# SwiGLU products by one level of Strassen's recursion in a two-layer decoder step

## The chip, the cores and the metric

The kernel runs on one core of one Trainium2 chip. The metric is the device time of one execution in microseconds; the median of three runs is taken.

## The reference, cut to what matters

One inference step of a two-layer decoder for 1024 prompt tokens and 8 x 8 sample tokens, model width 1024, all in float32. Layer 0 mixes tokens by trailing means over 2 to 16 positions, layer 1 by dilated attention in three branches over a shared K/V. Each layer ends with a SwiGLU:

```python
def _swiglu(h, w_gate, w_up, w_down):
    return (jax.nn.silu(h @ w_gate) * (h @ w_up)) @ w_down
...
        xp = xp + _swiglu(_rmsnorm(xp, ffn_norm[layer]), w_gate[layer], w_up[layer], w_down[layer])
        xs = xs + _swiglu(_rmsnorm(xs, ffn_norm[layer]), w_gate[layer], w_up[layer], w_down[layer])
```

The hidden width D_FF is 2816. The caches of the sample tokens are also copied to the outputs, shifted by the new rows.

## The kernel before, in words

The engines are TensorE (PE, whose weight loads are shown as PEld), VectorE (DVE), ScalarE (ACT), GpSimd (POOL) and SyncE (SP, which issues most DMAs). Prompt and sample tokens stand side by side as T = 1088 columns. The residual stream `xall` is kept feature-major, 8 tiles of 128 features by 1088 tokens.

Every float32 operand of a large product is split (`split`, L195) into a high part, ACT's cast to fp32r (L196), and a low part, DVE's subtraction (L197). `mm3` (L199) makes a product of three matmuls from them: high x high, high x low, low x high (L200 to L202). Each matmul loads its own 128 x 128 weights.

A SwiGLU (`ffn`, L358) runs over 22 chunks of 128 hidden features and, inside, over the three token groups of 364, 362 and 362 columns in `GROUPS`. `load` brings a chunk's gate, up and down weights and splits them. `gate_up` (L373) makes 2 x 8 products into two PSUM banks, then ACT's Silu (L384), DVE's product (L385) and a split of the result. `down` (L391) makes eight products, one for each 128 output features, and DVE adds each from PSUM onto `xall` (L399). `norm` (L317) makes the normed stream of a group: ACT squares, DVE adds (L332), a matmul with ones, the reciprocal root, DVE's scaling (L353) and a split. Layer 0's norm of a group is called by the pool mixer as soon as that group is mixed, and its last groups are split for the projections (`split_stream`, L431) while others still run. The output projection (L1000 to L1008) goes over the same three groups.

The order on an engine is made by a scheduler from the program's order and its own costs, except on POOL within a SwiGLU, where it is the program's. `copy_some` (L163) has POOL issue the next cache copies (168 in all, about 1 MB each, HBM to HBM); each waits for the last matmul made before it. In the SwiGLUs before, POOL does nothing else. In attention POOL has products of its own (L902) and casts (L754).

SBUF holds three raw weight tiles (`raw_tile`) and twelve split ones (`split_tile`, `wide_tile`); PSUM's eight banks are shared by tags (`FFN_PS`: s 3, p 2, o 1, a 2).

## Time and profile before

| what | us |
|---|---|
| median of the three runs | 3244.33 |
| lowest, highest run | 3237.19, 3258.73 |
| span of the profiled execution | 3241.6 |

The profile is of one execution. Its span goes from the first to the last instruction; no other time of that execution is given, and the three runs lie on both sides of it. Matmuls are pipelined: their records overlap, so the time that one costs is read from how many start in a stretch, not from the length of a record. By stage: the pool mixer to about 85 us, the first SwiGLU to 907, the projections to 1756, attention to 2330, the output projection to 2422, the second SwiGLU and the outputs to the end.

### The profile page before, as it was taken

Reading aid. Unit: us, or ns where it says so; the run is one execution under the profiler, and the core shown is the slowest. Engines: PE = TensorE matmul, PEld = TensorE weight load, DVE = VectorE, ACT = ScalarE, POOL = GpSimd, SP = SyncE. Lnnn points to the kernel's source line nnn. Section 1 sums busy time; section 2 is a strip of 40 time slices with the busy share of each in tenths; the row PEclk is TensorE's granted clock in tenths of the full one; section 3 lists DMA queues with packets and bytes.
Section 4 is the critical chain, followed back from the end, with each engine's and each line's share of the span. In section 5 each row is a group of like instructions: output and inputs, shape, how many; then the busy total and the mean of one; then the engine's idle time right before and its main releaser. Section 6 shows DMA issues by size and latency. Waiting matters only on the chain.

```text
span 3241.6 us, 50563 instructions
## 1 busy us (share of the span) xinstructions
PE 3191.2 (98%) x18673; PEld 2943.7 (91%) x18673; DVE 2144.0 (66%) x4692; ACT 1194.6 (37%) x3907; POOL 207.4 (6%) x463
## 2 busy tenths in 40 slices
PE   8999999999999999999998999999999999999998
PEld 7999999999978888888887888888999999999998
DVE  6655555555689999799892677687636555555555
ACT  5311111111255565253442677777523111111111
POOL 1000000000000000000000012132100000000000
PEclk9999999999999999999998999999999999999999
DMA  4444454445446676978977667776424455445431
GB/s 131 151 162 159 152 172 162 160 149 175 143 146 203 229 226 215 323 266 289 317 218 204 181 225 253 232 260 213 167 67 149 156 175 163 148 155 173 160 118 56
DMA packets 250140, 599.75 MB, mean 185 GB/s; under 512 B 24190, under 2 KB 128174, under 8 KB 246069
## 3 DMA queue, kind: packets, MB, share of 16 engines
q1 hardware_dynamic: 216167, 368.89, 36.3%
q0 software_dynamic: 5376, 174.60, 15.4%
q10 hardware_dynamic: 28350, 53.03, 4.5%
q8 instruction: 147, 2.41, 0.3%
q14 instruction: 100, 0.82, 0.1%
HBM read 534.51 MB, written 243.56 MB: 240 GB/s over the span
## 4 chain that ended last, share of the span: by engine, by line
PE 96%; DVE 2%; DMA 1%; ACT 1%; issue 0%; SPq 0%; DVEq 0%; ACTq 0%
PE ps_s L200 9%; PE ps_s L202 9%; PE ps_s L201 9%; PE ps_p L201 8%; PE ps_p L200 8%; PE ps_p L202 8%; PE ps_o L200 5%; PE ps_o L201 5%; PE ps_o L202 5%; PE ps_a L201 4%; PE ps_a L200 4%; PE ps_a L202 4%; PE ps_s L827 4%; PE ps_o L860 3%; PE ps_p L852 2%; PE ps_a L757 2%
## 5 line engine op out<-in xcount | busy, mean ns | idle before, releaser
L399 DVE TENSOR_TENSOR xall<-xall,ps_s 128x362 f32<-128x362 f32 (+1 forms) x1056 | 546.3, 531 | 582.2 <-PE ps_s L202 575.8
L196 ACT CAST wsplit<-wraw 128x1024 fp32r<-128x1024 f32 x142 | 149.0, 1050 | 654.5 <-PE ps_s L201 270.8
L200 PE MATMUL ps_p<-yah,wsplit 128*128 128x362 f32 (+1 forms) x1104 | 363.5, 329 | 0.2
L201 PE MATMUL ps_p<-yal,wsplit 128*128 128x362 f32 (+1 forms) x1104 | 362.6, 330 | 0.6 <-DVE yal L197 0.4
L202 PE MATMUL ps_p<-yah,wsplit 128*128 128x362 f32 (+1 forms) x1104 | 362.7, 329 | 0.0
L200 PE MATMUL ps_s<-hh,wsplit 128*128 128x362 f32 (+1 forms) x1056 | 349.5, 332 | 6.6 <-DVE xall L399 4.0
L201 PE MATMUL ps_s<-hl,wsplit 128*128 128x362 f32 (+1 forms) x1056 | 348.4, 330 | 0.0
L202 PE MATMUL ps_s<-hh,wsplit 128*128 128x362 f32 (+1 forms) x1056 | 348.3, 330 | 0.0
L200 PE MATMUL ps_o<-yah,wsplit 128*128 128x362 f32 (+1 forms) x752 | 248.4, 330 | 0.0
L201 PE MATMUL ps_o<-yal,wsplit 128*128 128x362 f32 (+1 forms) x752 | 247.3, 329 | 0.0
L202 PE MATMUL ps_o<-yah,wsplit 128*128 128x362 f32 (+1 forms) x752 | 247.1, 329 | 0.0
L201 PEld LDWEIGHTS ps_p<-yal,wsplit 128*128 128x128 f32 x1104 | 208.5, 189 | 1.7 <-DVE yal L197 1.6
L200 PEld LDWEIGHTS ps_p<-yah,wsplit 128*128 128x128 f32 x1104 | 209.0, 189 | 0.5 <-ACT yah L196 0.4
L202 PEld LDWEIGHTS ps_p<-yah,wsplit 128*128 128x128 f32 x1104 | 208.8, 189 | 0.0
L200 PEld LDWEIGHTS ps_s<-hh,wsplit 128*128 128x128 f32 x1056 | 199.0, 189 | 10.1 <-DVE xall L399 6.7
L197 DVE TENSOR_TENSOR wsplit<-wraw,wsplit 128x1024 fp32r<-128x1024 f32 x142 | 173.5, 1222 | 41.0 <-ACT wsplit L196 40.9
L202 PEld LDWEIGHTS ps_s<-hh,wsplit 128*128 128x128 f32 x1056 | 200.0, 189 | 0.0
L201 PEld LDWEIGHTS ps_s<-hl,wsplit 128*128 128x128 f32 x1056 | 199.8, 189 | 0.2
L384 ACT ACTIVATE sl<-ps_p 128x364 f32<-128x364 f32 (+1 forms) x132 | 62.3, 472 | 324.0 <-PE ps_p L202 324.0
L838 ACT ACTIVATE S<-S,ml 128x128 f32<-128x128 f32 (+1 forms) x384 | 169.1, 443 | 28.3 <-DVE ml L833 26.1
L167 POOL DMA_DIRECT2D out_kv_sample<-in_cache_kv_w x168 | 81.6, 488 | 1518.2 <-PE ps_o L202 1054.1
L196 ACT CAST hh<-sl 128x364 fp32r<-128x364 f32 (+1 forms) x132 | 65.3, 494 | 302.7 <-PE ps_s L202 260.6
(290 smaller groups left out, 7486.2 us busy)
## 6 DMA issues: line engine op xcount, KB each, us to landing
sqb<-q SPq DMA_DIRECT2D x128, 512.0 KB
vc<-in_cache_kv_w SPq DMA_DIRECT2D x208, 256.0 KB
skt<-in_cache_kv_w SPq DMA_DIRECT2D x96, 512.0 KB
wraw<-in_w_kv SPq DMA_DIRECT2D x48, 512.0 KB
out_kv_sample<-in_cache_kv_w POOLq DMA_DIRECT2D x24, 960.0 KB, 7.5
wraw<-in_w_gate SPq DMA_DIRECT2D x44, 512.0 KB
wraw<-in_w_up SPq DMA_DIRECT2D x44, 512.0 KB
wraw<-in_w_down SPq DMA_DIRECT2D x44, 512.0 KB
```

The source lines that it names most:

```text
L167: c = bulk.dma_start(_raw(kv_s[b], (n * WIN[b] + r) * row, [[row, m], [1, row]]), _raw(caches[b], (n * WIN[b] + r + TS) * row, [[row, m], ...
L196: nc.scalar.copy(h, x)
L197: nc.vector.tensor_sub(l, x, h.bitcast(FT))
L200: nc.tensor.matmul(out, wh, xh, start=first, stop=False)
L201: nc.tensor.matmul(out, wh, xl, start=False, stop=False)
L202: mark[0] = nc.tensor.matmul(out, wl, xh, start=False, stop=last).ins
L399: nc.vector.tensor_add(xT[m][:, o:o + n], xT[m][:, o:o + n], p[:, :n])
L757: nc.tensor.matmul(acc, w, vl, start=e == 0, stop=False)
L827: nc.tensor.matmul(ps[hh][:, c:c + 128], self.qT[hs, jj, :], kt[hs, jj, :], start=True, stop=True)
L838: nc.scalar.activation(subs[hh][:, e], subs[hh][:, e], AF.Exp, bias=self.ml[:, 0, h:h + 1], scale=-1.0, accum_out=self.ml[:, 1, h:h + 1])
L852: nc.tensor.transpose(pp[:, e * 128:(e + 1) * 128], Sf[:, e * 128:(e + 1) * 128], ident)
L860: nc.tensor.matmul(self.po[:, h % 8 * 64:h % 8 * 64 + 64], Ps[hh][:, c:c + 128], vv[:, h * 64:(h + 1) * 64], start=z == 0, stop=z == nb - 1)
```

## The change

With A the weights, transposed, and B the normed stream, cut into 2 x 2 blocks, one level of Strassen's recursion (in Winograd's form) makes the four result blocks from seven block products and sums of blocks. For gate and up, A is cut by pairs of hidden chunks (11 pairs) and by halves of the features, B into forms of 4 x 128 features by 272 tokens. The 1088 tokens are four blocks of NB = 272; blocks 0 and 1 are the left half (B11, B21), 2 and 3 the right one, and an index g goes over the two blocks of a half. The forms B11, B21, B22 and T1 to T4 are made once per layer by `forms_one` and `forms_two` and kept split. The forms of A are made for each unit (a pair and "gate" or "up"). The gated blocks are stored to scratch HBM (`hd`) and the SwiGLU's whole gate/up part runs before its down part, which loads them again for each of its seven products and forms sums on POOL. In down, a product fills all eight PSUM banks over 11 chunks, and its result is added to one or more blocks of the stream, which has been stored to HBM before the gate/up part and is loaded again. The down weights are loaded afresh for each product. The cache copies are issued three per unit in gate/up and three at chunks 3 and 7 of each down product, until they are used up.

The projections read the stream back from HBM in tiles and take the token tiles in the order `TORD`, those of blocks 2 and 3 first. The split weight tiles are ten instead of twelve; the projections and the output projection get four of their own. The pool mixer's groups become 384, 384 and 320 tokens, its tiles a pool of their own.

The diff, cut to the new order and the functions that set it:

```diff
-GROUPS = ((0, 364), (364, 362), (726, 362))
+STR_PS = {"f": 8}
+NSPLIT = 10
+NB = T // 4
+NPAIR = NFF // 2
+AHEAD = 3
+TORD = (5, 6, 7, 8, 0, 1, 2, 3, 4)
...
+    def norm(q, gain, tag):
+        w = wide_tile()
+        sq = [w[:, :NB], w[:, NB:2 * NB]]
+        acc = w[:, 2 * NB:3 * NB]
+        for k in range(8):
+            xk = xall[:, k, q * NB:(q + 1) * NB]
+            if k == 0:
+                nc.scalar.activation(acc, xk, AF.Square)
+                continue
+            nc.scalar.activation(sq[k % 2], xk, AF.Square)
+            nc.gpsimd.tensor_add(acc, acc, sq[k % 2])
...
+        r = wide_tile()[:, :NB]
+        nc.scalar.copy(r, p[:, :NB])
+        for k in range(8):
+            xk = xall[:, k, q * NB:(q + 1) * NB]
+            nc.vector.scalar_tensor_tensor(xk, xk, gain[:, k:k + 1], r, op0=OP.mult, op1=OP.mult)
+    def quarter(kh, q):
+        return xall[:, 4 * kh:4 * kh + 4, q * NB:(q + 1) * NB]
+
+    def forms_one(X, g):
+        split(*X["B11", g], quarter(0, g))
+        split(*X["B21", g], quarter(1, g))
+
+    def forms_two(X, g):
+        y11, y12, y21, y22 = quarter(0, g), quarter(0, g + 2), quarter(1, g), quarter(1, g + 2)
+        split(*X["B22", g], y22)
+        nc.vector.tensor_sub(y11, y12, y11)
+        split(*X["T1", g], y11)
+        nc.gpsimd.tensor_sub(y12, y22, y12)
+        nc.vector.tensor_sub(y22, y22, y11)
+        split(*X["T2", g], y22)
+        split(*X["T3", g], y12)
+        nc.gpsimd.tensor_sub(y21, y22, y21)
+        split(*X["T4", g], y21)
...
+    STEPS = ("A11", "A12", "S2", "S3", "S1", "A22", "S4")
+    MATE = {"A11": "B11", "A12": "B21", "S4": "B22", "A22": "T4", "S1": "T1", "S2": "T2", "S3": "T3"}
...
+    def gate_up(layer, X, pl, hd, ncopy):
...
+        def prep(n, f):
+            if n >= len(UNITS):
+                return
+            if f == "A11":
+                load(n)
+            (a11, a21), (a12, a22) = ((r[:, :, 0:128], r[:, :, 128:256]) for r in RAW[n])
+            if f == "S2":
+                s = wide_tile().rearrange("p (z k f) -> p z k f", z=2, k=4)
+                nc.vector.tensor_add(s[:, 0], a21, a22)
+                nc.vector.tensor_sub(s[:, 1], s[:, 0], a11)
+                SUM[n, "S1"], SUM[n, "S2"] = s[:, 0], s[:, 1]
+                s = wide_tile().rearrange("p (z k f) -> p z k f", z=2, k=4)
+                nc.vector.tensor_sub(s[:, 0], a11, a21)
+                nc.vector.tensor_sub(s[:, 1], a12, SUM[n, "S2"])
+                SUM[n, "S3"], SUM[n, "S4"] = s[:, 0], s[:, 1]
+            if f in ("A11", "A12") and n < 2 * EARLY:
+                return
+            src = {"A11": a11, "A12": a12, "A22": a22}[f] if f[0] == "A" else SUM[n, f]
+            F[n, f] = split_form(src)
+        def product(p, n, f, g, first, last):
+            h, l = F[n, f]
+            xh, xl = X[MATE[f], g]
+            for k in range(4):
+                mm3(p[:, :NB], h[:, k], l[:, k], xh[:, k], xl[:, k], first and k == 0, last and k == 3, skip_group_check=True)
+        def take(n, b, g, src, other=None, op=None):
+            c, nm = UNITS[n]
+            if nm == "g":
+                s = SG[c, b][:, g]
+                if other is None:
+                    nc.scalar.activation(s, src, AF.Silu)
+                else:
+                    nc.vector.tensor_tensor(s, other, src, op=op)
+                    if g:
+                        nc.scalar.activation(SG[c, b], SG[c, b], AF.Silu)
+            else:
+                s = SG[c, b]
+                if other is None:
+                    nc.vector.tensor_mul(s[:, g], s[:, g], src)
+                else:
+                    if g == 0:
+                        U[n, "t"] = pl.tile([128, 2, NB], FT, name="ct", bufs=2)
+                    t = U[n, "t"]
+                    nc.vector.tensor_tensor(t[:, g], other, src, op=op)
+                    if g:
+                        nc.gpsimd.tensor_mul(s, s, t)
+                if g:
+                    sync.dma_start(hd[b, c], s.rearrange("p g t -> p (g t)"))
+        def one(n):
...
+            pa = [bank("f") for g in range(2)]
+            for g in range(2):
+                product(pa[g], n, "A11", g, True, True)
+                nc.scalar.copy(u[:, g], pa[g][:, :NB])
+            for g in range(2):
+                product(pa[g], n, "A12", g, False, True)
+                take(n, "B11", g, pa[g][:, :NB])
...
+        def rest(n, j, pb):
...
+                p = pb[g] if f == "S4" else bank("f")
+                if f == "S1":
+                    pb.append(p)
+                product(p, n, f, g, f != "S4", True)
+                s = p[:, :NB]
+                if f == "S2":
+                    nc.vector.tensor_add(u2[:, g], u2[:, g], s)
+                elif f == "S3":
+                    nc.vector.tensor_add(u3[:, g], u2[:, g], s)
+                elif f == "S1":
+                    take(n, "B22", g, s, u3[:, g], OP.add)
+                elif f == "A22":
+                    take(n, "B21", g, s, u3[:, g], OP.subtract)
+                else:
+                    take(n, "B12", g, s, u2[:, g], OP.add)
...
+        for n in range(2 * EARLY):
+            load_early(n)
+        for j in range(7):
+            prep(0, STEPS[j])
+        for n in range(2 * EARLY):
+            one(n)
+            copy_some(ncopy)
+        for n in range(len(UNITS)):
+            pb = []
+            for j in range(7):
+                prep(n + 1, STEPS[j])
+                if j == 0:
+                    if n >= 2 * EARLY:
+                        one(n)
+                    if n >= 2 * EARLY:
+                        copy_some(ncopy)
+                elif j > 1:
+                    rest(n, j, pb)
+    DOWN = (("A11", "B11"), ("S1", "T1"), ("S2", "T2"), ("S4", "B22"), ("S3", "T3"), ("A12", "B21"), ("A22", "T4"))
+    def down(layer, kp, hp, hd, ncopy, after):
...
+        def prep(n):
+            if n >= 7 * NPAIR:
+                return
+            s, c = divmod(n, NPAIR)
+            fa, fb = DOWN[s]
+            if fa == "A11":
+                src = two(s, c, 0, 0)
+            elif fa == "S1":
+                r = wraw(c, 0, 1, 2, 128 * D)
+                src = SK[c] = kp.tile([128, 512], FT, name=f"sk{c}")
+                nc.gpsimd.tensor_add(src, r[:, 0], r[:, 1])
+            elif fa == "S2":
+                src = SK[c]
+                nc.gpsimd.tensor_sub(src, src, two(s, c, 0, 0))
...
+            t = split_tile()
+            W[n] = t[:, :512], t[:, 512:]
+            split(*W[n], src)
+            if fb == "T1":
+                TK[c] = kp.tile([128, 2 * NB], FT, name=f"tk{c}")
+                src = TK[c]
+                nc.gpsimd.tensor_sub(src, hraw("B12", c), hraw("B11", c))
...
+            t = hp.tile([128, 2, 2 * NB], FR, name="hf", bufs=4)
+            Hf[n] = t[:, 0], t[:, 1]
+            split(*Hf[n], src)
...
+        for s, (fa, fb) in enumerate(DOWN):
+            pb = [bank("f") for _ in range(8)]
+            for c in range(NPAIR):
+                n = s * NPAIR + c
+                prep(n + AHEAD)
+                (wh, wl), (xh, xl) = W.pop(n), Hf.pop(n)
+                for i in range(4):
+                    for g in range(2):
+                        m, t = slice(i * 128, i * 128 + 128), slice(g * NB, (g + 1) * NB)
+                        mm3(pb[2 * i + g][:, :NB], wh[:, m], wl[:, m], xh[:, t], xl[:, t], c == 0, c == NPAIR - 1)
+                if c in (3, 7):
+                    copy_some(ncopy)
+            for i in range(4):
+                for g in range(2):
+                    p, u = pb[2 * i + g][:, :NB], uu[:, 2 * i + g]
+                    x11, x12, x21, x22 = (xall[:, i + 4 * z, (g + 2 * t) * NB:(g + 2 * t + 1) * NB]
+                                          for z in range(2) for t in range(2))
+                    if fa == "A11":
+                        nc.scalar.copy(u, p)
+                        nc.gpsimd.tensor_add(x11, x11, u)
+                    elif fa == "S1":
+                        nc.vector.tensor_add(x22, x22, p)
+                        nc.vector.tensor_add(x12, x12, p)
+                    elif fa == "S2":
+                        nc.vector.tensor_add(u, u, p)
+                        nc.gpsimd.tensor_add(x12, x12, u)
...
+            if fa == "S3":
+                after(1)
+            elif fa == "A22":
+                after(0)
+    def swiglu(layer, X, xa, xs, npool, last, after):
...
+        with pool("g1") as pl:
+            gate_up(layer, X, pl, hd, 3)
+        npool.close()
+        xa.close()
...
+            for q in (0, 2, 1, 3):
+                sync.dma_start(blk(xall, q), xs[q])
+            down(layer, kp, hp, hd, 3, after)
+            last()
...
+    def mixed(gi):
+        if gi == 1:
+            spill("x0", (0, 1), x0)
+            for g in range(2):
+                norm(g, G_F0, "s")
+                forms_one(X, g)
...
+    spill("x0", (2, 3), x0)
+    X.update(form_tiles(xb.enter_context(pool("xb", side="left")), ("B22", "T1", "T2", "T3", "T4")))
+    for g in range(2):
+        norm(g + 2, G_F0, "s")
+        forms_two(X, g)
+    xr.close()
+    psum_shares(STR_PS)
+    swiglu(0, X, xa, x0, xb, lambda: None, lambda half: spill("x1", (2 * half, 2 * half + 1), x1))
...
-        for o, n in GROUPS:
+            for q in range(4):
+                t = slice(q * NB, (q + 1) * NB)
...
+                if m4 and q < 2:
+                    spill("x2", (q,), x2)
+                    norm(q, G_F1, "s")
+                    forms_one(X, q)
...
```

## Rows read from the trace of the kernel before

**Rows 1.** The page: busy time by engine, and the chain by engine.

```profile
PE 3191.2 (98%) x18673; PEld 2943.7 (91%) x18673; DVE 2144.0 (66%) x4692; ACT 1194.6 (37%) x3907; POOL 207.4 (6%) x463
...
PE 96%; DVE 2%; DMA 1%; ACT 1%; issue 0%; SPq 0%; DVEq 0%; ACTq 0%
```

**Rows 2.** Windows by stage; the columns are named in the first line.

```profile
core 0: us, PE busy (x) PEld busy (x) DVE busy (x) ACT busy (x) POOL busy (x), PEclk, DMA share, GB/s
85.00:112.00 27.00, 25.64 (x136) 24.18 (x136) 23.82 (x52) 14.70 (x28) 0.67 (x1) 0.88 0.37 117
112.00:150.00 38.00, 38.00 (x233) 37.99 (x232) 21.08 (x47) 12.33 (x22) 2.43 (x5) 1.00 0.51 166
150.00:870.00 720.00, 720.00 (x4345) 720.00 (x4344) 378.02 (x664) 119.41 (x185) 39.67 (x82) 1.00 0.49 161
870.00:907.00 37.00, 30.14 (x148) 25.93 (x148) 34.95 (x52) 13.11 (x16) 0.00 (x0) 0.91 0.33 105
...
2422.00:2428.00 6.00, 0.81 (x8) 0.73 (x7) 4.92 (x16) 5.09 (x9) 0.00 (x0) 0.88 0.53 157
2428.00:2460.00 32.00, 31.42 (x172) 30.40 (x172) 30.28 (x75) 18.22 (x39) 1.04 (x2) 0.86 0.20 67
2460.00:3180.00 720.00, 720.00 (x4346) 720.00 (x4345) 374.73 (x659) 118.45 (x184) 37.77 (x78) 1.00 0.47 154
3180.00:3241.60 61.60, 51.89 (x331) 49.55 (x329) 34.32 (x67) 9.04 (x16) 0.00 (x0) 0.98 0.19 73
```

**Rows 3.** Windows of the projections, same columns.

```profile
1100.00:1700.00 600.00, 600.00 (x2644) 490.95 (x2643) 552.52 (x1093) 277.38 (x1380) 0.00 (x0) 1.00 0.78 262
1500.00:1700.00 200.00, 200.00 (x882) 163.68 (x881) 182.95 (x306) 83.64 (x363) 0.00 (x0) 1.00 0.84 285
```

**Rows 4.** Groups by line and shape, whole span: xcount | busy us, mean ns | idle before.

```profile
L399 DVE TENSOR_TENSOR xall<-xall,ps_s 128x362 f32<-128x362 f32 x704 | 363.3, 531 | 415.2 <-PE ps_s L202 410.8
L200 PEld LDWEIGHTS ps_p<-yah,wsplit 128*128 128x128 f32 x1104 | 209.0, 189 | 0.5 <-ACT yah L196 0.4
L197 DVE TENSOR_TENSOR wsplit<-wraw,wsplit 128x1024 fp32r<-128x1024 f32 x142 | 173.5, 1222 | 41.0 <-ACT wsplit L196 40.9
L196 ACT CAST vh<-vc 128x512 fp32r<-128x512 f32 x208 | 122.2, 615 | 60.9 <-DMA vc<-in_cache_kv_w 31.4 <-PE ps_a L758 22.4 <-PE ps_a L757 3.1
L902 POOL TENSOR_TENSOR wraw<-wraw,mw 128x1024 f32<-128x1024 f32 x16 | 32.7, 2063 | 84.6 <-DVE mw L899 84.2 <-DMA mm<-ml 0.4
L353 DVE SCALAR_TENSOR_TENSOR nf<-xall,gcol,nr 128x362 f32<-128x362 f32 x32 | 18.5, 592 | 1.3 <-ACT nr L350 1.1
```

**Rows 5.** Timeline of attention: start us, us, engine line op, xcount.

```profile
2131.55 5.30 DVE L197 TENSOR_TENSOR vl<-vc,vh 128x512 fp32r<-128x512 f32 x3
...
2131.72 4.59 POOL L902 TENSOR_TENSOR wraw<-wraw,mw 128x1024 f32<-128x1024 f32 x2 [0.61 <-DVE mw L899]
...
2201.30 1.98 PEld L860 LDWEIGHTS ps_o<-wsplit,P 128*128 128x128 f32 x16
...
2202.07 0.69 DVE L197 TENSOR_TENSOR vl<-vc,vh 128x512 fp32r<-128x512 f32 x1
...
2202.24 4.60 POOL L902 TENSOR_TENSOR wraw<-wraw,mw 128x1024 f32<-128x1024 f32 x2 [0.45 <-DMA mm<-ml]
2203.09 1.99 DVE L197 TENSOR_TENSOR vl<-vc,vh 128x512 fp32r<-128x512 f32 x1 [0.32 <-ACT vh L196]
...
2205.00 0.41 DVE L833 CUSTOM_DVE_ANT_0 S<-ps_s,amask 128x256 f32<-128x256 f32 x1
```

**Rows 6.** The page: the DMA queue of the cache copies.

```profile
q0 software_dynamic: 5376, 174.60, 15.4%
```

**Rows 7.** Window of the prompt's attention, columns as in the windows above.

```profile
1850.00:2330.00 480.00, 476.12 (x3535) 406.42 (x3534) 359.85 (x1115) 351.18 (x1025) 111.84 (x284) 0.99 0.66 218
```

More of the change, by code (lines that the diff above doesn't have):

```diff
@@ L32 @@
 NVAL = NS * 2 * 13
-NT = 'a'
-ON_PE = False
 TURN = 3
@@ L55 @@
 VALUE_SPAN = 96
-TILES_OF = ((0, 1), (2, 3, 4), (5, 6, 7, 8))
 def _constants():
@@ L1013, in output @@
+    ystack.close()
+    spill("x2", (2, 3), x2)
+    X.update(form_tiles(xb.enter_context(pool("xb1", side="left")), ("B22", "T1", "T2", "T3", "T4")))
+    for g in range(2):
+        norm(g + 2, G_F1, "s")
+        forms_two(X, g)
+    xr.close()
+    psum_shares(STR_PS)
+    def output():
+        for i in TORD:
             o, n = TILES[i]
-            y = pl.tile([128, D], FT, name="y", bufs=3)
+            y = wide_tile()
             for h2 in range(2):
-                p = bank("s" if i > 4 and h2 else "p")
+                p = bank("f")
@@ L1024, in output @@
             sync.dma_start(dst, y[:n])
-    with pool("ffn1") as pl:
-        for gi in range(3):
-            norm(gi, pl, yh, yl, G_F1)
-        ffn(1, yh, yl, pl, (1, 1, 2), lambda gi: output(pl, TILES_OF[gi]))
+    swiglu(1, X, xa, x2, xb, output, lambda half: None)
     copy_some(len(copies_left))
```

439 lines of the change are left out of this document (220 added, 219 removed).

## Prediction

> **What bounds the kernel now.** I read the page's sums first. TensorE (PE) is busy 98% of the span, and the chain that ended last lies 96% on PE [rows 1]. The windows by stage show where: in the two steady SwiGLU stretches PE is busy all of 720.00 us, with 4345 and 4346 matmuls, while VectorE (DVE) is at 52%, ScalarE (ACT) at 17% and the DMA engines at half [rows 2]. So a SwiGLU costs what its matmuls cost, one every 720.00 / 4345 = 165.7 ns, for moving operands of 364, 362 and 362 columns (mean 362.7). The profiled execution's span is 3241.6 us; the median of the three runs, 3244.3, is 2.7 us above it. The sum below is made against the span and 2.7 is added at the end. About 1% (32 us) is what a measurement of this kernel can tell from no change.
>
> **The matmuls, the term with the minus sign.** Before, a layer's SwiGLU has 22 x (16 + 8) products x 3 passes x 3 groups = 4752 matmuls. After: gate and up 22 units x 7 products x 2 token halves x 4 k x 3 passes = 3696, down 7 x 11 chunks x 8 banks x 3 = 1848, together 5544 of 272 columns. Columns fall by an eighth (1,723,392 to 1,507,968), instructions rise by a sixth, so all depends on what one of 272 costs. No row has that size with this type. Two rows span the nearest: 362.7 columns at 165.7 ns, and 512 columns, in the projections, at 600.00 / 2644 = 226.9 ns [rows 3]. The line through them has 0.410 ns a column and 17 ns a matmul; at 272 it gives 128.6 ns. Bounds: 272/362.7 of 165.7, that is 124.3 ns, if all of it scaled, and 165.7 if none did. I take 128.6, since both rows lie on it. Two layers: 9504 x 165.7 = 1574.8 against 11088 x 128.6 = 1425.9 us: **-149**. The output projection goes from three groups to four blocks: 576 x 165.7 = 95.4 to 768 x 128.6 = 98.8: **+3**.
>
> The Trainium skill, "TensorE: Matmul & The Clock Gate", section "Back-to-back issue gap", gives columns / 2.4 + 2.5 ns for a warm matmul by itself. At 272 that would be 115.8 ns, and the sum 142 us lower; but it would also give 153.6 and 215.8 ns for the two sizes above, 11 to 12 ns under both measured ones, so the sum goes by the rows.
>
> **The start of each SwiGLU.** Before, a group's norm is followed by its matmuls. After, only B11 and B21 (token blocks 0 and 1) serve the early products of four units, 4 x 48 x 128.6 ns = 24.7 us of PE work; the rest waits for T1 to T4, which need all four blocks. The work in that wait: per pair of a block of each half, a norm has 7 adds of 272 on POOL and 8 scalings on DVE, and forms_two has 7 DVE operations of 1088 elements and 2 on POOL. From the rows (DVE 531 ns at 362 and 1222 at 1024 elements, 592 for a scaling of 362, POOL 2063 at 1024 [rows 4]) these are 7 x 0.55 + 8 x 0.50 + 7 x 1.29 + 2 x 2.19 = 21.3 us. They add, rather than overlap, because DVE with two operands in SBUF stands still while POOL runs a tensor operation: a subtraction that takes 0.69 us took 1.99 us beside POOL's product, and three took 5.30 us beside two, while the DVE operation that reads PSUM kept its 0.41 us [rows 5]. Two pairs are 42.6 us; with 5 us to get going, 23 us are uncovered. Layer 0 has about 6 us of unfinished mixer on top: 29. Before, this start lost 14 us (85 to 150 us: 369 matmuls x 165.7 = 61 of 65 us, and some 10 us' worth of those are mixer work or transposes [rows 2]): **+15**. In layer 1 blocks 2 and 3 are projected last, 24.7 us of PE work under which norms 0 to 2 go; 11 us uncovered and 5.5 for the first weights, against 9.5 lost now (2422 to 2460: 172 x 165.7 = 28.5 of 38 us): **+7**. Ends for both together: -10 if the scheduler interleaves well, +55 if nothing overlaps.
>
> **Gate and up, steady.** A unit is 168 x 128.6 ns = 21.6 us on PE. DVE has 4 sums and 7 low parts of 512 elements at 0.69 and 10 to 12 of 272 at 0.44: 12.0 to 12.8 us, POOL three products of 544 in every second unit, 3.3 us. It fits. A12 accumulates onto A11's bank after ACT has copied it: queued behind that copy are ACT's casts (0.62 each), with 1.5 us of slack. **+8** for both layers (0 to 30).
>
> **From gate/up to down.** The gated blocks go to HBM and come back; the first three chunks are long there, the reload of the stream (4.4 MB) is in the same SP queue. If SP issues it first, the chunk loads stand behind it for 4.4 MB at 339 GB/s, 13 us. **+6** for both (0 to 30).
>
> **Down: the DVE/POOL port.** A chunk is 24 matmuls, 3.09 us. In the products S1, S2 and S3 each chunk needs DVE's two low parts (0.69 + 0.72) and POOL's two differences (512 and 544 elements, 1.03 + 1.10): 3.54 us in sequence, by [rows 4, 5]. 33 chunks x 0.45 = 15 us a layer; POOL's adds after A11 and S2 (16 x 0.55) come on top, three prepared chunks (9.3 us) cover most. The other products need 1.4 to 2.5 us and fit. With PSUM evictions between products (8 to 16 DVE operations of 0.44 us against 3 us until PE is round the 8 banks) I take 14 a layer: **+28** (0 if the exclusion is partial, 70 if each step adds 0.2 us of hand-over and every S1 eviction shows).
>
> **Down of layer 0: the DMAs.** copy_some(3) twice per product puts 42 of the 168 cache copies (174.6 MB in all [rows 6], 1.04 MB each) here; layer 1's down has none, as its gate/up takes the last 60. S1 and S3 load 11 x (2 x 262 + 2 x 278.5 KB) = 11.9 MB; with 6.2 MB of copies, 18.1 MB. The busiest stretch moved 285 GB/s at 0.84 busy, 339 when full [rows 3]: 53.5 us against 38.9 by the port, 29 us over two products; the other five lack 2 us each. Nothing waits for the copies, so 0 to 39; I take **+20**.
>
> **The ends.** Layer 0's SwiGLU now ends with 12 us lost (870 to 907: 148 matmuls are 24.5 of 37 us [rows 2]), the stream split by DVE. After, blocks 2 and 3 are final two products earlier, and the projections begin with their tiles, 4 x 24 x 226.9 ns = 21.8 us of PE work, while blocks 0 and 1 go out and back: 7 lost, **-5** (-12 to +10). The tail after layer 1 stays about 11 us (3180 to 3241.6): 0. Two weight buffers fewer in attention, where PE waits 4 of 480 us now [rows 7]: **+3** (0 to 10).
>
> **Sum:** 3241.6 - 149 + 3 + 15 + 7 + 8 + 6 + 28 + 20 - 5 + 3 = 3177.6; + 2.7 = **3180 us**.
>
> **The rivals.**
> *The port and the copies don't show* (three chunks of lead and late copies absorb them, and the starts are covered): without +28, +20 and 15 of the starts, 3117. For it: DVE is half idle now. Against: [rows 5], every instance blocks. 0.14.
> *Down is bound everywhere*: hand-overs of 0.2 us and all evictions (+42 more), the copies in full (+19), 10 more at the starts: 3251, no change. For it: seven products a layer with a barrier of 8 banks each. Against: nothing of that size stalls PE now. 0.22.
> *The weight load sets the pace* (slower): 128.6 ns needs a load hidden under 272 columns. A load is recorded at 189 ns [rows 4], longer than the whole new spacing. 11088 matmuls make 61 us of gain vanish at 134.1 ns; from there the change loses, at 140 ns 3306 us. Against it: behind 64-column matmuls 16 loads came in 1.98 us, at most 0.12 each [rows 5], though of plain f32. 0.08. The Trainium skill, same page, "Part 3: Packing small matmuls", section "The mechanism", says a load overlaps running matmuls only in other row groups. All row groups are used here; its load of 107 ns ("LDWEIGHTS") plus 113 of streaming would be an estimated 220 ns and some 1000 us more. By it 362.7 columns would already cost 258 ns; [rows 2] has 165.7.
> The forecast's own case, 3130 to 3225, has 0.56.
>
> **Chances and range.** Of the forecast's 0.56, 0.03 lies above 3212 (1% under 3244); with the first rival, faster is 0.67. No change: that 0.03 and most of the second rival, 0.22. Slower: the load and the second rival's far end, 0.11. Range 3100 to 3262: from a little under the first rival to the second one's with its bounds; outside are the load and a few hundredths below.
>
> **What would show it.** In steady gate/up the spacing is 128 to 129 ns with 5544 matmuls a layer; at 134 or more the last rival has it. At each SwiGLU's start PE idles some 15 to 30 us in all. In down, S1, S2 and S3 take 37 to 40 us against 34 for A12, and their first waits end on DVE low parts behind POOL differences; layer 0's S1 and S3 are longer than layer 1's, at full DMA. If layer 0's and layer 1's down take the same, the copies cost nothing. If idle of PE is more than 90 us over the two SwiGLUs, the forecast is too low.

## The result, and the profile after

The changed kernel takes 3371.82 us (median of 4 runs, 3361.77 to 3373.17) against 3248.36 us before (median of 4, 3237.19 to 3258.73): ratio 1.0378, 95% interval 1.0348 to 1.0407. It is slower by 3.8%; 3180 us were forecast, faster by 2%. The profiled execution has a span of 3359.8 us, 118.2 more than the one before. One profiled execution further down, e11's, took 4997.6 us at a granted clock of 0.55 throughout, and its time and profile are left out.

The page of the changed kernel, busy time by engine, and the queue of the cache copies:

```profile
PE 3084.4 (92%) x20467; PEld 2801.2 (83%) x20467; DVE 2321.8 (69%) x4621; ACT 1406.6 (42%) x4340; POOL 733.0 (22%) x833
...
q0 software_dynamic: 5376, 174.60, 14.7%
```

PE has 107 us less work than before [rows 1] in a longer span: 275 us without work instead of 50. Where these lie is seen in the windows by stage (columns in the first line). The bounds are the events themselves: 85 is the old start of the first SwiGLU, 226 the first B22 product, 655 the end of gate and up, 977 the end of down; then the projections, the output projection (from 2446), and the second SwiGLU with its start (2555), gate and up (2656) and down (3085).

```profile
core 0: us, PE busy (x) PEld busy (x) DVE busy (x) ACT busy (x) POOL busy (x), PEclk, DMA share, GB/s
85.00:150.00 65.00, 36.93 (x165) 33.22 (x165) 39.25 (x67) 21.24 (x40) 22.37 (x17) 0.58 0.12 39
150.00:226.00 76.00, 40.96 (x289) 40.03 (x290) 36.94 (x56) 20.98 (x37) 17.15 (x14) 0.77 0.69 229
226.00:655.00 429.00, 429.00 (x3411) 429.00 (x3412) 262.58 (x450) 127.15 (x231) 74.37 (x85) 1.00 0.63 212
655.00:977.00 322.00, 256.87 (x1847) 250.88 (x1846) 193.57 (x205) 94.01 (x159) 180.56 (x164) 0.89 0.90 320
977.00:997.00 20.00, 0.74 (x2) 0.50 (x2) 11.98 (x26) 4.94 (x7) 0.00 (x0) 0.59 0.99 275
1100.00:1700.00 600.00, 599.35 (x2571) 476.28 (x2570) 547.14 (x1104) 276.11 (x1430) 0.00 (x0) 1.00 0.78 264
...
2555.00:2656.00 101.00, 43.52 (x309) 41.73 (x308) 59.49 (x85) 30.73 (x54) 31.66 (x23) 0.72 0.55 183
2656.00:3085.00 429.00, 429.00 (x3410) 429.00 (x3411) 267.45 (x457) 129.66 (x235) 73.37 (x80) 1.00 0.60 201
3085.00:3345.00 260.00, 242.99 (x1859) 237.59 (x1858) 190.77 (x199) 87.71 (x149) 177.47 (x121) 0.97 0.63 203
```

Two windows inside the steady stretches give the spacing of 272 columns:

```profile
250.00:640.00 390.00, 390.00 (x3114) 390.00 (x3114) 246.18 (x417) 119.94 (x219) 67.50 (x78) 1.00 0.64 215
2700.00:3080.00 380.00, 380.00 (x3035) 380.00 (x3034) 237.04 (x399) 116.73 (x213) 66.23 (x75) 1.00 0.64 215
```

390.00 / 3114 = 125.2 ns, and 380.00 / 3035 is the same. So the matmuls gain more than forecast: 11088 x 125.2 = 1388.2 against 1574.8 us, -187. Gate and up run without a gap, as before [rows 2]. All of the loss lies around them. With 125.2 ns as the price of a SwiGLU matmul, the stages against those before give:

| stage | forecast, us | measured, us | how measured |
|---|---|---|---|
| matmuls of both SwiGLUs | -149 | -187 | spacing |
| start of layer 0 | +15 | +89 | first B22 product at 225.8 less 288 matmuls x 125.2, against 85 + 15.6 of other work and waits before |
| start of layer 1 | +7 | +52 | first B22 product, less the same 288, is 64.7 behind the output projection's end, against 13.0 lost before |
| gate and up, both | +8 | +5 | 429 us against 3408 x 125.2 |
| down of layer 0 and the way to it | about +37 | +90 | 321.7 us against 1848 x 125.2 = 231 |
| down of layer 1 and the way to it | about +17 | +28 | 259.2 against 231 |
| layer 0's end to the projections | -5 | +7 | PE idle 19.7 us, against 13 lost before (870 to 907) |
| projections | 0 | +30 | +24 of it spacing: 233.3 ns for 226.9, 3744 matmuls |
| output projection | +3 | +9 | 109.3 against 99.9 us |
| attention, tail | +3 | -5 | -2, and 15.8 us behind the last SwiGLU matmul against 10.5 and 8.7 lost ahead of it before |
| sum | -64 | +118 | spans |

What held PE in the first start, from the waits of 120 to 230 us (engine, tile and line that waited, what for: total, times, longest):

```profile
DVE wsplit L398 <- DMA wraw<-in_w_gate: 28.8, 1, 28.8
...
PE ps_f L202 <- DVE sg L423: 25.2, 1, 25.2
...
PE ps_s L228 <- POOL wsplit L224: 17.7, 2, 14.8
...
PE ps_f L202 <- ACT u L449: 9.4, 1, 9.4
```

PE's longest wait, 25.2 us, names a DVE sum, but DVE itself stood 28.8 us before a gate weight. Beside it, on POOL's timeline, lie the copies of the early units:

```profile
179.82 1.64 POOL L169 DMA_DIRECT2D out_kv_sample<-in_cache_kv_w  x3 [10.99 <-PE ps_f L204]
182.83 1.44 POOL L169 DMA_DIRECT2D out_kv_sample<-in_cache_kv_w  x3 [1.37 <-PE ps_f L204]
185.86 1.44 POOL L169 DMA_DIRECT2D out_kv_sample<-in_cache_kv_w  x3 [1.59 <-PE ps_f L204]
189.51 0.49 POOL L169 DMA_DIRECT2D out_kv_sample<-in_cache_kv_w  x1 [2.21 <-DMA out_kv_sample<-in_cache_kv_w]
192.41 0.49 POOL L169 DMA_DIRECT2D out_kv_sample<-in_cache_kv_w  x1 [2.41 <-DMA out_kv_sample<-in_cache_kv_w]
196.76 0.49 POOL L169 DMA_DIRECT2D out_kv_sample<-in_cache_kv_w  x1 [3.86 <-DMA out_kv_sample<-in_cache_kv_w]
```

Twelve copies of 1.04 MB within 17 us, while the early products last 4 x 48 x 125 ns = 24 us: 12.5 of the 17.4 MB (229 GB/s x 76 us) that the window of 150 to 226 us moved.

### The profile page after: what moved, and what is told of

Read it like the earlier page. It is cut to its first block, busy times and chain, and to the rows that moved or that the text cites. A ratio compares the mean times of both kernels' runs of the same rounds, so it can differ in the third digit from the quotient of the medians.

```text
span 3359.8 us, 56006 instructions
## 1 busy us (share of the span) xinstructions
PE 3084.4 (92%) x20467; PEld 2801.2 (83%) x20467; DVE 2321.8 (69%) x4621; ACT 1406.6 (42%) x4340; POOL 733.0 (22%) x833
## 5 line engine op out<-in xcount | busy, mean ns | idle before, releaser
L203 PE MATMUL ps_f<-hf,wsplit 128*128 128x272 f32 x1232 | 359.6, 299 | 32.6 <-DVE hf L199 32.6
L202 PE MATMUL ps_f<-hf,wsplit 128*128 128x272 f32 x1232 | 323.2, 296 | 46.1 <-ACT hf L198 22.4
L204 PE MATMUL ps_f<-hf,wsplit 128*128 128x272 f32 x1232 | 351.3, 298 | 3.1 <-DVE wsplit L199 3.1
L203 PEld LDWEIGHTS ps_f<-hf,wsplit 128*128 128x128 f32 x1232 | 243.6, 198 | 38.0 <-DVE hf L199 37.8
L202 PEld LDWEIGHTS ps_f<-hf,wsplit 128*128 128x128 f32 x1232 | 225.2, 196 | 50.8 <-ACT hf L198 23.9
L204 PEld LDWEIGHTS ps_f<-hf,wsplit 128*128 128x128 f32 x1232 | 240.5, 198 | 4.1 <-DVE wsplit L199 4.0
L199 DVE TENSOR_TENSOR wsplit<-wraw,wsplit 128x512 fp32r<-128x512 f32 (+1 forms) x228 | 186.2, 826 | 51.0 <-ACT wsplit L198 45.9
L199 DVE TENSOR_TENSOR wsplit<-wsplit 128x512 fp32r<-128x512 f32 x176 | 141.7, 808 | 96.6 <-ACT wsplit L198 96.4
L199 DVE TENSOR_TENSOR vl<-vc,vh 128x512 fp32r<-128x512 f32 x208 | 143.6, 716 | 44.5 <-ACT vh L198 43.5
L710 DVE TENSOR_TENSOR spr<-skt,sqb 128x1024 f32<-128x1024 f32 x128 | 154.6, 1208 | 21.3 <-DMA sqb<-q 19.1
L711 DVE TENSOR_REDUCE sc<-spr 128x16 f32<-128x1024 f32 x128 | 154.1, 1204 | 0.9
L1091 PE MATMUL ps_o<-wsplit,P 128*128 128x64 f32 x1120 | 145.4, 271 | 0.0
L1058 PE MATMUL ps_s<-akT,aqT 64*128 64x128 f32 x1120 | 145.4, 303 | 0.0
L1091 PEld LDWEIGHTS ps_o<-wsplit,P 128*128 128x128 f32 x1120 | 141.1, 194 | 5.1
```

Of the source, the lines that this page charges most:

```text
L199: nc.vector.tensor_sub(l, x, h.bitcast(FT))
L202: nc.tensor.matmul(out, wh, xh, start=first, stop=False, **kw)
L203: nc.tensor.matmul(out, wh, xl, start=False, stop=False, **kw)
L204: mark[0] = nc.tensor.matmul(out, wl, xh, start=False, stop=last, **kw).ins
L710: nc.vector.tensor_mul(pr, kt, qb)
L711: nc.vector.tensor_reduce(sc[b][:, :, n * TS + t], pr.rearrange("p (h d) -> p h d", d=HD), axis=AX.X, op=OP.add)
```

## Experiments: where the forecast's terms went

Each is one execution beside one of the kernel before, unless said; stage lengths are compared between profiles of the same program parts. Whole executions of one kernel differ by some 10 us (3361.77 to 3373.17 for the changed one), so the argument rests on the stages. The first four change the changed kernel in one place each.

**e1: no copies among the early products.**

```diff
         for n in range(2 * EARLY):
             one(n)
-            copy_some(ncopy)
...
-                        copy_some(ncopy)
+                        copy_some(ncopy + (n < 16))
```

> The twelve cache copies that the four early units issue in a burst are moved to units 4 to 15 (four each instead of three); the number per layer stays. Theory A (the burst's 12.5 MB stands before the small packets of the next gate and up weights, and PE waits for these): the two waits of 25.2 us (at 200.6) and 24.5 us (at 2631.4) before B22's first product fall to under 5 us each, and the span falls by 35 to 50 us to about 3310 to 3325. Rival B (the wait is for the forms and splits on DVE, ACT and POOL, which only end late): both waits stay above 20 us and the span within 10 us of 3360.

Measured: span 3299.0, 61 less. Its windows of both starts and of gate and up:

```profile
150.00:200.40 50.40, 40.62 (x289) 39.91 (x290) 38.07 (x57) 21.45 (x38) 11.17 (x2) 0.85 0.36 106
200.40:627.60 427.20, 427.20 (x3411) 427.20 (x3411) 265.92 (x447) 127.20 (x230) 80.48 (x97) 1.00 0.71 242
...
2521.40:2599.00 77.60, 45.74 (x308) 44.02 (x307) 60.75 (x87) 31.27 (x55) 25.80 (x11) 0.74 0.27 83
```

The same 289 matmuls take 50.4 us for 76, the start of layer 1 77.6 for 101. That is 49 us, and both waits of 25 us are gone; the rest of the 61 lies in pieces of 2 to 4 us in other stages. The moved copies cost gate and up nothing. The start was not only a question of what DVE and POOL do: with the copies its DMA engines stood at 0.69, without them at 0.36.

**e2: no copies in down** (its 42 go to gate and up, 18 to layer 0's and 24 to layer 1's, one more per unit).

```diff
-                        copy_some(ncopy)
+                        copy_some(ncopy + 1)
...
-                if c in (3, 7):
-                    copy_some(ncopy)
```

> Layer 0's down part issues no cache copies; they go to gate and up of both layers (four per unit instead of three, from unit 4 on). Theory A (copies and loads share the DMA engines, and layer 0's down is late by the copies): layer 0's down falls from 321.7 us to layer 1's 259 (within 10), and the span by 55 to 70 us to about 3290 to 3305, if gate and up stay at 429 us. Rival B (the DVE and POOL port alone makes it late, the copies lag without harm, as 0 of my 0 to 39 us): it stays above 305 us. Rival C (the copies harm gate and up instead): its 429 us rise by more than 20.

Measured: span 3304.9, 55 less. The window of layer 0's down:

```profile
654.80:920.70 265.90, 242.76 (x1849) 238.99 (x1847) 194.91 (x211) 96.14 (x162) 177.80 (x122) 0.96 0.71 233
```

265.9 us for 321.7: the copies cost 55.8 us there, beyond the 39 that the forecast had as its upper bound. With them the DMA engines moved 320 GB/s at a share of 0.90, without them 233 at 0.71. Most of the loss lies where the forecast expected the copies to show, in S1 (72.4 us in layer 0, 41.2 in layer 1) and S3 (51.5 and 35.0). S1 of layer 0 and of layer 1 in the changed kernel:

```profile
692.00:764.40 72.40, 41.75 (x266) 40.88 (x265) 43.19 (x28) 17.13 (x29) 49.87 (x43) 0.75 0.90 324
...
3118.40:3159.60 41.20, 36.55 (x265) 34.95 (x266) 31.78 (x23) 14.53 (x27) 41.20 (x29) 0.96 0.77 250
```

**e3: down's sums on DVE instead of POOL.**

```diff
-                nc.gpsimd.tensor_add(src, r[:, 0], r[:, 1])
+                nc.vector.tensor_add(src, r[:, 0], r[:, 1])
...
```

> In down, the eight sums and differences of weights and gated blocks are made by DVE instead of POOL; the additions onto the stream stay on POOL. Theory A (POOL and DVE shut each other out of SBUF, 3.5 us a chunk in S1, S2 and S3): on DVE alone the same work is 0.69 + 0.72 + 0.69 + 0.72 = 2.8 us against 24 x 0.125 = 3.0 us on PE, so layer 1's down (no copies in it) falls from 259 us towards 231 to 245, and the span by 14 to 40 us. Rival B (the barriers of eight PSUM banks between products, with DVE's evictions, make the loss): DVE gets fuller and layer 1's down stays within 6 us of 259 or grows.

Measured: span 3316.3, 43 less, of which attention and the output projection, which the edit does not touch, are 10. Layer 0's down takes 302.2 for 321.7, layer 1's 248.4 for 259.2. DVE does more work and the stage is shorter. That POOL is merely slower at the sums would not explain it, for DVE's own low parts were held: the same 33 in layer 1's down took 1495 ns each beside POOL's sums (first line, the changed kernel) and 748 ns without them (second line, e3).

```profile
L199 DVE TENSOR_TENSOR wsplit<-sk,wsplit 128x512 fp32r<-128x512 f32 x33 | 49.0, 1495 | 11.3 <-ACT wsplit L198 10.2
...
L199 DVE TENSOR_TENSOR wsplit<-sk,wsplit 128x512 fp32r<-128x512 f32 x33 | 24.7, 748 | 1.0 <-ACT wsplit L198 0.7
```

The Trainium skill, "SBUF — State Buffer", section "Who interferes with whom", says that a DVE instruction with two SBUF inputs and a GpSimd instruction that reads SBUF shut each other out; the 1495 against 748 ns agree.

**e4: the token tiles of the projections as two wide tiles.**

```diff
-    Y = {i: [ypool.tile([128, 8, 128], FR, name=f"y{c}{i}") for c in "hl"] for i in TORD if i < 8}
+    ya = [ypool.tile([128, 8, SP], FR, name=f"yw{c}") for c in "hl"]
+    Y = {i: [a[:, :, i * 128:(i + 1) * 128] for a in ya] for i in TORD if i < 8}
```

> The split stream that the projections read as weights lies in two wide tiles of 8 x 1024 columns, as in the kernel before (8 x 1088), instead of sixteen tiles of 8 x 128. Theory A (how the weights lie in SBUF sets the few ns per matmul beside the columns): the spacing of the 512-column matmuls falls from 233.3 ns to 226.8 as before, and the projections by about 3456 x 6.5 ns = 22 us. Rival B (it is where the tiles lie, on the other side of SBUF, or the DMA traffic beside them): the spacing stays at 233. The start of the projections may come later by some us, as one tile waits for all that lay in its place.

Measured: span 3360.6, spacing 233.3 ns as in the changed kernel, PE's idle time at the boundary 19.6 us. The form of the stationary tiles is not what made 512 columns slower.

**e5: the copies spread, and e3's edit.** One copy after each of four or five block products of units 4 to 21, 84 a layer, none elsewhere.

```diff
...
                 elif j > 1:
                     rest(n, j, pb)
+                    if n >= 2 * EARLY and (j < 6 or n < 16):
+                        copy_some(1)
...
```

> The changed kernel with two edits together: the cache copies are issued one at a time after the block products of units 4 to 21 of gate and up (84 a layer, none among the four early units and none in down), and down's differences and sums of the stream are made by DVE instead of POOL. Theory A: the losses found singly add up: the two waits of about 25 us at the starts go (150.3 to 225.8 us becomes about 150 to 200 in layer 0, 74 us to 51 in layer 1), down of layer 0 falls from 321.7 us by 55 (copies) and 11 to 20 (port) to about 250, down of layer 1 from 259 to about 248. Span 3220 to 3240 us. Rival B: 84 copies a layer beside the gate and up weights make these late, gate and up grow from 429 us by 10 or more each, and the span stays at 3250 or above.

Measured: span 3221.8; 3223.57 against 3244.47 us for the kernel before on the same chip, one run each. Gate and up and down of layer 0:

```profile
202.90:630.10 427.20, 427.20 (x3412) 427.20 (x3411) 271.84 (x454) 129.51 (x234) 90.67 (x116) 1.00 0.82 285
630.10:883.20 253.10, 239.99 (x1849) 237.94 (x1847) 181.05 (x293) 93.66 (x159) 32.84 (x33) 0.96 0.73 243
```

The losses add as theory A had it. 84 copies beside the weights bring the DMA engines to 0.82 and PE waits for nothing.

**e6: the norms' adds and two of the forms on DVE, both norms ahead of the forms** (on top of e5).

```diff
-            nc.gpsimd.tensor_add(acc, acc, sq[k % 2])
+            nc.vector.tensor_add(acc, acc, sq[k % 2])
...
     for g in range(2):
         norm(g + 2, G_F0, "s")
+    for g in range(2):
         forms_two(X, g)
...
```

> As e5_base, and the norm's seven adds a block and the two POOL differences of forms_two go to DVE; norms 2 and 3 both stand before the two forms_two in the program. Theory A (DVE and POOL shut each other out, and the second norm's matmul with ones and its transposes, which stand ahead of the early products in PE's order, wait for the first forms): the early products begin earlier and cover the forms; from the first early matmul to the first B22 product 30 to 40 us instead of 50, and each start 10 to 25 us shorter, span 20 to 45 us under e5_base. Rival B: ACT's squares and casts set the pace of the start, under 8 us gained in all, or a loss because DVE gets 2 x 28 more adds.

Measured: span 3201.9, 20 less than e5, of which the starts have 11.5: the first B22 product comes 9.5 us earlier in layer 0 and 2 in layer 1, and from the first early product to it are still 47.2 us for 50.2. So neither holds as it was put: the gain is over B's 8 us, but layer 0's start gained just under A's 10 to 25 us and layer 1's 2, and the early products cover no more than before. Three things change at once here (the adds, the two forms, the order), and no run takes them apart. The second norm's matmul still waited 17.3 us, now for DVE.

**e7: norms 0 and 1 after the mixer** (on top of e5).

```diff
         if gi == 1:
             spill("x0", (0, 1), x0)
+        if gi == 2:
             for g in range(2):
```

> As e5_base, and the norms of blocks 0 and 1 of layer 0 are called after the last group of the mixer instead of after the second. Theory A: the first norm's matmul with ones stood ahead of the mixing of token tiles 6 to 8 in PE's order and held it (83 us): mixing ends 10 us or more earlier, and the first early product comes 5 to 15 us earlier than in e5_base. Rival B: norms 0 and 1 then are late instead, and all four come behind one another: the first early product comes at the same time or up to 15 us later. Layer 1 as in e5_base.

Measured: span 3218.0; the first early product at 145.3 us for 152.7, within A's range. The order on PE had cost 7 us of layer 0's start.

**e8: the last stores of the stream on ACT's queue** (on top of e5).

```diff
-            sync.dma_start(dst[q], blk(xall, q))
+            queue.dma_start(dst[q], blk(xall, q))
...
```

> As e5_base, and the store of blocks 0 and 1 of the stream at the end of layer 0's down is issued on ACT's queue instead of SP's. Theory A: SP, which waits with these stores for the last additions, held the loads of token tiles 5 to 8 behind them: PE's idle time before the first projection matmul falls from 16 to 20 us to under 10. Rival B: what the projection waits for is the stored stream itself or the splits, not SP's order: idle time unchanged within 3 us. In both cases the span differs from e5_base by no more than that.

Measured: PE waits 17.0 us before the first projection matmul, as without it (16.7): B. The waits at that boundary show another holder: ACT's casts into the extra weight tiles (px) wait for the store of the stream, whose memory they take, with the token splits (yh) behind them.

```profile
PE ps_o L202 <- ACT yh L198: 17.0, 1, 17.0
ACT px L738 <- DMA x<-xall: 15.1, 1, 15.1
```

**e9: everything on the right side of SBUF moved by 32 bytes** (on top of e5, e6 and e7).

```diff
+    shift = ctx.enter_context(tc.tile_pool(name="shift", bufs=1, side="right")).tile([128, 8], FT, name="shift")
+    nc.vector.memset(shift, 0.0)
     wpool = ctx.enter_context(tc.tile_pool(name="wpool", bufs=1, side="right", reuse_waits="tile"))
```

> e6_forms and e7_mixlate together (expected span 3192 to 3199 us by itself), and 32 bytes are taken at the end of SBUF ahead of the weight tiles, so that they, and all pools behind them, move by 32 bytes. In the kernel before, the projections' moving operands (the split weights) began at addresses that are multiples of 64 bytes, in the changed kernel 32 past one. Theory A: a 512-column matmul whose moving operand begins 32 bytes past such a multiple costs 6.4 ns more: the spacing in the projections falls from 233.3 to 226.9 ns and the projections from 881 to about 857 us; the 272-column matmuls on B11, B21 and the down operands gain about 1 ns each (126.5 to 125 in the changed kernel's own trace), some 3 us a layer; span 3160 to 3172. Rival B: the spacing has another cause (the order of the token tiles, the small weight pool of the projections): 233 ns stays, the span stays above 3190.

Measured: span 3189.1. A window of its projections:

```profile
1000.00:1600.00 600.00, 598.89 (x2634) 488.55 (x2633) 558.01 (x1132) 284.93 (x1491) 0.00 (x0) 1.00 0.78 266
```

598.89 / 2634 = 227.4 ns, close to the 226.9 of before [rows 3]; e10, without the shift, keeps 600.00 / 2574 = 233.1. The projections take 860.2 us for e6's 881.3. Only their moving operands had moved, the stationary ones are on the left side: A holds there. It fails for the 272 columns: gate and up, where the stationary weights moved and the moving operands of only two products in seven (B11, B21), went from 427.2 to 430.0 us a layer; by the starts of their matmuls, the five whose moving operands stayed went from 125.0 to 125.3 ns up to 126.1. Down, where both operands moved, kept its 124.7 ns. The span stayed above the range given, and only 7 us under e10's, whose own edit gained nothing: gate and up gave back 5 of the projections' gain, layer 0's start 4, and the stretch from the projections to layer 1's first product 7.5. That stretch took 693 to 705 us over the runs, so whether the shift lengthened it, or the start, is not shown.

**e10: px in a pool of its own, off the stream's memory** (on top of e5, e6 and e7).

```diff
-        with pool("proj") as pl:
+        with pool("projx") as px, pool("proj") as pl:
...
```

> e6_forms and e7_mixlate together, and the projections' four extra weight tiles (px) come from a pool of their own that doesn't lie on the memory of the stream. In the changed kernel these tiles lie where the stream lay, so ACT's first cast into one waits for the store of the stream to end (ACT waited 11 to 15 us for it), and the first token splits stand behind that cast on ACT. Theory A: with that wait gone, PE's idle time before the first projection matmul falls from 16 us to 7 to 11, where SP's loads of the token tiles set it; span 5 to 9 us less than it would be (3192 to 3199), so 3184 to 3193. Rival B: SP's issues of 1.2 to 2.1 us each set it alone, and the idle time stays within 2 us of 16.

Measured: span 3196.2, PE's wait at the boundary 18.3 us: B, if a little beyond its 2 us. ACT no longer waits for the store but 11.5 us for a weight load, and SP, after its weight loads and the tables, issues four token loads in 8.6 us:

```profile
ACT px L740 <- DMA wraw<-in_w_q: 11.5, 1, 11.5
```

```profile
871.88 8.58 SPq L678 DMA_DIRECT2D skt<-x  x4
```

Behind each holder stands another one almost as late. One thing is the same in all of these boundaries: the DMA engines are nearly full with the stores of the stream, its token loads and the next weights, 4.5 MB in e8 and 4.8 MB in e10 (first and second line), 5.5 MB in the changed kernel (its window of 977 to 997 us). In the kernel before, that stretch stood at 0.33 [rows 2].

```profile
878.50:895.50 17.00, 0.02 (x1) 0.02 (x1) 4.72 (x11) 3.49 (x5) 0.00 (x0) 0.62 0.97 264
...
863.60:882.00 18.40, 0.21 (x2) 0.00 (x0) 8.62 (x22) 2.35 (x3) 0.00 (x0) 0.58 0.89 262
```

**e11: the first token loads on ACT's queue** (on top of e9; four executions beside seven of the kernel before).

```diff
-                sync.dma_start(x[:, :, lo - o:hi - o], x1[q]
+                (store_q if i in TORD[:4] else sync).dma_start(x[:, :, lo - o:hi - o], x1[q]
```

> e9_align (3189.1 us), and the loads of the first four token tiles for the projections are issued on ACT's queue instead of SP's, where they stood behind weight loads, the rope table and the gains (issued 8 us after the SwiGLU's end in e10_px, landed after 17). Theory A: with the stream's blocks 2 and 3 in HBM two products earlier, these loads land before the SwiGLU ends and PE's idle time before the first projection matmul falls from 16 us to under 6: span 3176 to 3182, and 1.5 to 2.5% under the kernel before. Rival B: ACT's own order holds them (casts of down's last operands stand ahead), the idle time stays above 12 us and the span within 4 us of 3189.

Measured: 3188.2 us (median) against 3245.61, ratio 0.9817, interval 0.9793 to 0.9841: 1.8% faster than before, and no faster than e9 (3190.82, one run) beyond what executions differ by. Its wait at the boundary is not known, so only the time speaks, and it speaks for B.

**e12: the changed kernel's share of copies in down, but issued singly** (on top of e9).

```diff
-                if c in (3, 7):
-                    copy_some(ncopy)
+                if c in (1, 3, 5, 7, 8, 9):
+                    copy_some(1)
```

> e9_align, but with the changed kernel's shares of the cache copies: 42 in layer 0's down and 66 and 60 in gate and up; each is issued alone, in down after chunks 1, 3, 5, 7, 8 and 9 of each product instead of three at once after chunks 3 and 7. With bursts of three, down of layer 0 took 302 us (e3_port), without copies 248 (e9_align). Theory A (the bytes: down's own loads and the copies together need more than the DMA engines move): down of layer 0 takes 285 us or more. Rival B (the bursts: a copy's large packets hold up the small loads behind them only as long as several are queued): 250 to 265 us.

Measured: layer 0's down 297.1 us, 49 more than in e9 without copies. Its two windows, the first of gate and up with 66 copies, the second of down:

```profile
192.70:622.60 429.90, 429.90 (x3412) 429.90 (x3410) 271.57 (x454) 129.56 (x234) 81.51 (x98) 1.00 0.71 241
622.60:919.70 297.10, 248.35 (x1849) 243.76 (x1847) 181.37 (x291) 94.70 (x159) 53.31 (x75) 0.91 0.94 349
```

A: it is the bytes, not the bursts. 297.1 us at 349 GB/s are 103.7 MB; e3's down, with bursts, moved 302.2 x 344 = 104.0 MB at a share of 0.95. Issued either way, the same bytes keep the DMA engines full for about as long. The Trainium skill, "DMA: Bandwidth & Descriptors", section "Where 436 GB/s comes from", has some 358 GB/s as the HBM limit of one core. The means of 344 and 349 lie just under it, but fortieths of this stage (7.4 us) moved up to 486 GB/s, and a copy both reads and writes HBM, so no run here shows that limit.

**e13: norms 2 and 3 as a pair** (on top of e9; four executions beside seven of the kernel before). What was left open was the rest of the starts.

```diff
-    for g in range(2):
-        norm(g + 2, G_F0, "s")
+    norm_pair((2, 3), G_F0, "s")
...
+    def norm_pair(qs, gain, tag):
+        accs = [norm_sum(q) for q in qs]
...
+        rsqrt(rs, ss, ms, a, 1.0 / D)
+        for z, q in enumerate(qs):
+            norm_rest(q, gain, tag, rs[:, 3 * z:3 * z + 3], cols)
```

> e9_align (3189.1 us), and the norms of blocks 2 and 3 are made as a pair: both sums of squares first, one reciprocal root for both, then the scalings of both, then the forms. In e9_align DVE had the forms of the first pair between the adds of the second norm, and PE waited 17.2 us for that norm's matmul with ones, with the early products behind it in its order. Theory A (the late second norm holds the early products, and these would cover the forms): the 17.2 us go, the first early product comes 8 to 14 us earlier (144.1 to about 132; in layer 1 the same), and the first B22 product 8 or more earlier, in each layer; span 3165 to 3177. Rival B (the forms' end sets the start, since the A12 products need the u tiles, which lie on the stream's memory and are free only after the last form): the early A11 products come earlier, but PE's idle time ahead of the first A12 product (6.65 us) grows by as much, and the first B22 product gains under 5 us a layer; span 3180 or more.

Measured: 3188.15 us (median) against 3249.75, ratio 0.9815, interval 0.9784 to 0.9847. The first early product comes at 127.2 us for 144.1, and the first B22 product at 190.5 for 192.5: B. The waits of the start, and ACT's timeline at their end:

```profile
PE ps_f L204 <- ACT u L475: 17.5, 1, 17.5
```

```profile
157.25 1.10 ACT L200 CAST xT4h<-xall 128x1088 fp32r<-128x1088 f32 x1 [1.23 <-DVE xall L286]
160.85 0.62 ACT L200 CAST wsplit<-wsplit 128x512 fp32r<-128x512 f32 x1 [2.51 <-DVE wsplit L201]
163.86 2.41 ACT L475 COPY u<-ps_f 128x272 f32<-128x272 f32 x8 [2.39 <-DVE xT4l L201]
```

PE makes the A11 products of the four early units, 96 matmuls, into all eight banks and stops. Their copies to `u` all start when DVE has made the last form's low part (xT4l): `u` lies on the stream's memory, and that is the stream's last reader. So the early products cover 96 x 125 ns = 12 us of the forms, not 24, however early they begin.

## Why the forecast was wrong, point by point

**The matmuls.** Right in kind, 38 us too careful, which hid part of the other misses: 125.2 ns, near the lower bound of 124.3. From 362.7 down to 272 columns the slope is 0.447 ns a column, not the 0.410 of the line through 362.7 and 512. The rival of the weight load is out.

**"Nothing waits for the copies", +20.** This step failed, and it is the largest single piece: PE did wait, for the loads beside the copies, 36 us more than the +20 in down and 49 us at the starts, 85 of the 182 us by which the sum was off. It priced the copies only in down, product by product, took half of a bound of 39, and left out that the stream's reload and stores and the next stage's weights pass in the same stretch. By the sum of the stage's bytes it would have come out: the 103 MB that the trace has there (320 GB/s x 322 us), at the 339 GB/s that the step itself had, are 304 us, against the 252 (1848 x 128.6 + 14) that the matmuls and the port were given. Measured +55.8 (e2), and with down's sums on DVE +49, whether in bursts (e3 against e5) or singly (e12 against e9).

**The starts, +15 and +7.** Measured +89 and +52. The early copies were priced at nothing there: 49 us (e1). The early products were to cover the wait for the forms; instead they stand behind the second norm on PE, and when that is taken away they stop after half for want of memory (e13; in the changed kernel the same wait, for ACT's `u`, is 9.4 us). The adding up of POOL and DVE times was right in kind (in the changed kernel one of DVE's low parts of 1088 took 3.52 us beside POOL's difference, others 1.29), but taking it away gave little: e6, which takes POOL out and changes the order too, brought the first B22 product 9.5 us earlier in layer 0, and e7's order on PE 7.0. The granted clock fell as well: a mean of 0.58 from 85 to 150 us, mostly the lower of its levels (1.2 GHz), which it fell to at 76 us, in a wait of 4.2 us for the mixer, and again at 124, among the waits of a norm, and 0.85 in e1's window behind that, whose 289 matmuls took 40.6 us of PE (140 ns each). About 54 us of layer 0's start and 23 of layer 1's remain in e13. Their largest piece, by the timeline, is the chain of scalings and forms on DVE, busy from 125.9 to past 163 us without a break; no run shortened that chain, so that it sets the rest is not shown.

**The port in down, +28.** Right in mechanism and nearly in size: moving the sums to DVE took 10.8 us from layer 1's down and, once the copies were gone, 265.9 - 253.1 = 12.8 from layer 0's.

**The way from gate and up into down, +6,** was not measured by itself: 248 us of e13's down against 231 leave 17 a layer, with chunk loads and the sums between products in it; no run separates these.

**The ends, -5.** Wrong in sign: +7, 19.7 us of PE's idle time for the 13 lost before. That blocks 2 and 3 are in HBM two products early helps nothing, since their loads are issued only after the SwiGLU, behind weight loads and tables. Three edits, each of one holder, left 17 to 18 us or the same time. What the boundaries share is a DMA share of 0.89 to 0.99 while 4.5 to 5.5 MB pass, the same account as in layer 0's down; no run took bytes away there, so whether the bytes or the chain of holders sets the wait stays open.

**Not in the sum:** the 32 bytes of the weight tiles, 21 us of the projections (e9). The forecast had the new pools' order, but no row of before has such a tile at another address.

**The rivals.** "Down is bound everywhere" (3251) came nearest to the 3372 measured, by its copies in full and its longer starts; its hand-overs and evictions everywhere do not show as such, for layer 1's down, without copies, lost 28 us where the forecast had 17 and this rival 38. The forecast's own mark, over 90 us of PE idle in the two SwiGLUs, was passed: 128 us between 85 and 977, and 74 between 2555 and 3345.

## What to carry to other kernels

Sum the bytes of each stage, with everything that merely passes through it, against the rate of the stage before pricing a background copy at nothing: the same 42 copies cost 56 us in down, where the DMA engines then stood at 0.90, and nothing in gate and up, where they stood at 0.63 before taking them. When a block scheme makes the first products wait for all inputs, ask of the work meant to cover the wait where it stands in its engine's order and whose memory its outputs take. With the copies placed in gate and up, down's sums on DVE, the norms reordered and the tiles shifted, one level of Strassen's recursion does pay a little here: 3188.15 us, 1.8% under the kernel before (interval 1.5 to 2.2%), which is 62 of the 187 us that its matmuls save.

## What was not expected of the hardware

The start address of a moving operand: with 512 columns, 32 bytes past a multiple of 64 cost about 6 ns a matmul (233.1 against 227.4 in e10 and e9), while with 272 columns the shift back to such a multiple, there mainly of the stationary weights, cost 0.8 ns (427.2 to 430.0 us over 3412 matmuls). Only this one shift was tried. And a matmul of 272 columns in fp32r comes every 125.2 ns beside a weight load of its own that is recorded at 198 ns.
